# Half of the first slice's modulation product on TensorE with a one-column moving operand, between the transposes of x

## The chip, the cores and the metric

The kernel runs on one core of a Trainium2 chip. The metric is the time of one execution on the device in microseconds (us); smaller is better.

## The reference, cut to what matters

One decoder layer on 256 tokens of width 2048, in float32:

```python
mod = silu(c) @ w_ada + b_ada                       # (1, 2048) @ (2048, 6 * 2048)
sh1, sc1, g1, sh2, sc2, g2 = split(mod, 6)
h = rms_norm(x, norm1_gain) * (1.0 + sc1) + sh1
x = x + g1 * hybrid_mixer(h, ...)                   # begins with h @ w_in, 2048 x 16984
h = rms_norm(x, norm2_gain) * (1.0 + sc2) + sh2
x = x + g2 * swiglu(h, ...)
return rms_norm(x, final_norm_gain)
```

The change is in `silu(c) @ w_ada`, the product that makes the modulation, and there in a quarter of the columns of `sh1` and `sc1` alone. No other part of `w_ada` is touched.

## The kernel before

All large products run on TensorE with the contraction on the 128 partitions. A weight matrix comes from memory in chunks of four row tiles of 128 by 512 columns, 1 MB each. ScalarE casts a chunk, in halves, into its float32r part (`act.copy(hv, src)`, L303), VectorE subtracts that for the rest (L305), and TensorE makes three products for each row tile and token tile (L345 to L347): 24 for a chunk. The list `items` gives the order of the work, and `run()` walks through it; it also issues the loads on the SP queue in the order of the list, as far as there are free tiles named `raw`, three in each of two rings. A chunk is split two chunks ahead of its products.

The first products need `h`, and so the first norm and its modulation. To start early, the first 12 groups of `w_in` columns are done in four slices of four row tiles of the contraction (`INIT_KTS`), and each slice needs only its 512 columns of `sh1` and of `sc1`. Row 16p + j of `w_ada` lies on partition p. So a slice's part of `w_ada` is 16 rows for each partition, two times 512 columns wide, and it comes as eight pieces (`Ada`) of two rows `j` each, 1 MB, in two transfers of 512 KB, one for `sh1` and one for `sc1`. The tile `sc` holds silu(c) with a column for each `j`. VectorE works each piece into an accumulator `a`, by `pre_ada`: the product of a row with its column of `sc` (L283 for the very first row, a fused multiply-add L285 after it). What is left is a sum over the partitions, and the result must lie along partitions, as a column for each block of 128: `init_columns` calls `column_sums`, in which TensorE transposes the eight blocks of the accumulator (L481) and VectorE sums along the rows (L482). Three small VectorE operations (`mod_columns`, L455 to L457) make `A1` and `B1` of it.

Ahead of that stands the first norm (`first_norm`): ScalarE squares x and scales it in place (L451). Then `transpose_x` transposes it, 32 transposes of 128x128 on TensorE (L491), and ScalarE copies the result back in eight pieces (L495). `first_slice` then issues the casts of the first weight chunk (both halves, before all that follows on ScalarE), `init_columns`, and `init_modulate`, which makes `h` for four row tiles: ScalarE its float32r part (L464), VectorE a float32 copy (L468) and the rest (L471), with the halves of the first chunk's L305 between them.

Before the change the order at the start is: norm, all 32 transposes, the eight pieces (the last one worked segment by segment, `by_seg`, so that the transposes of the first segment can start early), `first_slice`, and the first products. The pieces of the later slices are spread between the groups of products.

Of the kernel before, what the change touches and what calls it, by code (L numbers as in the profile page):

```python
# [23 lines left out]
RAW_BUFS = 3          # raw chunks of weights in flight  # L24
EARLY_RAWS = 3        # and more of them while the working tiles of later stages are not there yet
HL_BUFS = 4           # halves of split chunks
AHEAD = 2             # chunks split ahead of their products
INIT_KTS = (4, 4, 4, 4)    # row tiles of the slices of the first products
ADA_DONE = 8          # the group of a slice before which the next slice's modulation is loaded and then applied
ADA_LEAD = (0, 2, 4)  # groups by which each slice's pieces of it start early  # L30
MID = 2               # row tile of the last chunk before which the first token tile's norm goes on
# The second norm's steps (512 columns, token tile) after the first two, with p for a half of a split,
# and the steps done before each row tile of the chunks that read them.
NORM_STEPS = "p 01 11 p p 20 21 30 31"
NORM_DONE = "0000 1233 3333 4557 7777 7777"
SLOT = 3.6            # vector engine time for the threads beside a chunk, in us
# [9 lines left out]
class Mm:  # L46
    """A chunk of a weight matrix: nk row tiles of 128, nc columns, for a group of products.

    With defer, the second token tile waits until a later chunk with by_token has done the first one.
    With home, its parts are in the tiles that home makes and not in the ring of all chunks.  # L50
    """
# [19 lines left out]
class Ada:  # L71
    """A piece of w_ada: nj of every partition's 16 rows, nc columns from c0 on of nseg segments."""

    def __init__(self, c0, nc, nseg, j0, nj, acc, pre=None):
        self.c0, self.nc, self.nseg, self.j0, self.nj, self.acc, self.pre = c0, nc, nseg, j0, nj, acc, pre
        self.by_seg = False

# [6 lines left out]
class Thread:  # L84
# [6 lines left out]
    def step(self):  # L91
        """The next step's cost, which it yields, or None at the end."""
        while True:
            if self.cur is None:
                if not self.q:
                    return None
                self.cur = self.q.popleft()
            try:
                return next(self.cur) or 0.0
            except StopIteration:  # L100
                self.cur = None
# [7 lines left out]
def tile_layer(tc, x, c, positions, norm1_gain, norm2_gain, w_ada, b_ada, w_in, gate_up, gate_bias,  # L109
# [3 lines left out]
    with (  # L113
# [42 lines left out]
        # ------------------------------------------------------------ constants and small inputs  # L156
# [36 lines left out]
        # rotary tables  # L193
# [22 lines left out]
        def rstd_of(ss, n, k):  # L216
            """(ss / n + eps) ^ -0.5 in place, k columns."""
            pool.tensor_scalar(ss, ss, 1.0 / n, EPS, ALU.mult, ALU.add)
            pool.tensor_tensor(ss, ss, half[:, 0:k], ALU.pow)

        def mean_of_three(ss):
            """ss[:, :, 0] becomes the part of mean + eps of the first three of four sums, for last_rstd."""
            pool.tensor_tensor(ss[:, :, 0], ss[:, :, 0], ss[:, :, 1], ALU.add)
            pool.tensor_tensor(ss[:, :, 0], ss[:, :, 0], ss[:, :, 2], ALU.add)
            pool.tensor_scalar(ss[:, :, 0], ss[:, :, 0], 1.0 / D, EPS, ALU.mult, ALU.add)
# [5 lines left out]
        # ------------------------------------------------------------ the stream of weights  # L231
# [42 lines left out]
        def pre_ada(it):  # L274
            if it.pre:
                it.pre()
            a = it.acc()
            segs = [slice(i, i + 1) for i in range(it.nseg)] if it.by_seg else [slice(0, it.nseg)]
            for g in segs:
                for j in range(it.nj):  # L280
                    s = sc[:, it.j0 + j:it.j0 + j + 1]
                    if it.j0 + j == 0:
                        dve.tensor_scalar_mul(a[:, g], it.raw[:, j, g], s)  # L283
                    else:
                        dve.scalar_tensor_tensor(a[:, g], it.raw[:, j, g], s, a[:, g], ALU.mult, ALU.add)  # L285
                    yield

        def pre_mm(it, rests_last=False):
            """The float32 chunk into its float32r part and the exact rest, a step for each half."""
            it.hl = []  # L290
            nk, ncol = (KT, 128) if isinstance(it, Lr) else (it.nk, it.nc)
            per = min(nk, 1024 // ncol)
            home = [h().rearrange("p (k n) -> p k n", k=nk) for h in getattr(it, "home", ())]
            rests = []
            for k in range(0, nk, per):
                src = it.raw[:, k:k + min(per, nk - k)]
                m = src.shape[1]
                if home:
                    hv, lv = (h[:, k:k + m] for h in home)
                else:  # L300
                    hv, lv = (stp.tile([128, 1024], F32R, tag=v, bufs=HL_BUFS, name=name(v))[:, 0:m * ncol]
                              .rearrange("p (k n) -> p k n", k=m) for v in ("hi", "lo"))
                act.copy(hv, src)  # L303
                it.hl.append((hv, lv))
                rests.append(lambda lv=lv, src=src, hv=hv: dve.tensor_sub(lv, src, hv.bitcast(F32)))  # L305
                if not rests_last:
                    rests.pop()()
                    yield
            for rest in rests:
                yield  # L310
                rest()

        def pre(its):
            """The pieces of its, a step of each in turn: steps of one piece of w_ada depend on each other."""
# [47 lines left out]
        def run():  # L362
# [36 lines left out]
            def pre_steps(**order):  # L399
                """The next chunk's pieces, a step at a time."""  # L400
# [38 lines left out]
        # ------------------------------------------------------------ first norm and its modulation  # L439
# [13 lines left out]
        def mod_columns(ps, n, A, B, bsc, bsh, gain):  # L453
            """A = (1 + scale) * gain and B = shift of n row tiles, from ps = [shift | scale]."""
# [4 lines left out]
        def modulated(kts, h, A, B, temp, on_act, between=None):  # L459
            """The transposed tokens in xs into the parts of h at the row tiles kts."""  # L460
# [14 lines left out]
        def column_sums(blocks, dst):  # L475
            """The sums of blocks [128, 128] over the partitions, a column of dst for each."""
# [7 lines left out]
        def transpose_x():  # L484
            """xs in place into its transposes, tiles [128, 256] for the row tiles; no block is overwritten before it is read."""
            pts = {}
            for k in range(0, KT, 2):
# [5 lines left out]
                for w in sorted(pts):  # L493
                    if min(2 * w + 4, KT) <= k + 2:
                        act.copy(xs[w // 8][:, (w % 8) * S:(w % 8 + 2) * S], pts.pop(w))  # L495

        def init_columns(s, k0, nk):
            a2 = init_acc(s, nk)
            pc = cp.tile([128, 2 * nk], F32, name=name("pc"))
            column_sums([a2[:, seg, a * 128:(a + 1) * 128] for seg in range(2) for a in range(nk)], pc)  # L500
# [48 lines left out]
        def first_transposes():  # L549
            first_norm()  # L550
            transpose_x()

        items.append(Call(first_transposes))
        items.extend(init_ada(*slices[0]))
        items[-1].by_seg = True
# [32 lines left out]
        # ------------------------------------------------------------ gated linear attention  # L588
# [179 lines left out]
        # ------------------------------------------------------------ indexer  # L768
        def rope(v, nh, dh, rot, step):
            """Rotates the first rot of dh in each of nh heads, in place, on both token tiles."""  # L770
# [100 lines left out]
        # ------------------------------------------------------------ sparse attention  # L871
# [3 lines left out]
        def seg_start(i):  # L875
            """Before the first piece of a segment: what the last one left is reduced."""
# [20 lines left out]
        def reduce_rows(dst, n):  # L897
            """A slice of 512 of the sums over the partitions added to dst, on every partition."""
# [112 lines left out]
        # ------------------------------------------------------------ branches, gates and merge  # L1011
# [32 lines left out]
        def split_transposes(src, kt0, dst):  # L1044
            """Transposes [128, 2, 512] into row tiles kt0.. of the parts in dst, in two steps."""
# [94 lines left out]
        # ------------------------------------------------------------ second norm  # L1140
        def second_norm(last):
# [17 lines left out]
            def modulate(n, t, ps, a0, na):  # L1159
                """Row tiles of one token tile; the second token tile's products are on the other engine."""  # L1160
# [61 lines left out]
        # ------------------------------------------------------------ feed-forward  # L1222
# [55 lines left out]
        def final_token(t):  # L1278
            """The last norm of a token tile; the columns before the last 512 have their gain already."""
# [54 lines left out]
def constants():  # L1334
    """Constants of the shapes alone: the identity, the masks of the decay's levels, the rotary frequencies."""
# [37 lines left out]
```

## Time and profile before

| what | value |
|---|---|
| time, median of 3 runs (lowest to highest) | 1889.79 us (1889.21 to 1892.36) |
| span of the profiled execution, first to last instruction | 1885.6 us |
| median less that span | 4.2 us |
| TensorE, busy share of the span | 97% |
| VectorE, ScalarE, GpSimd | 68%, 45%, 7% |
| memory traffic, mean over the span | 233 GB/s |
| granted TensorE clock, mean over the span | 0.995 of full speed |

The trace gives the span only; what lies around it in the execution's own time is not in the profile, so the last difference is taken for it. A busy time is the time in which an engine had an instruction in work. Times in the trace count from the first instruction.

### The profile page before, as it was taken

To read this page: it belongs to the slowest core of one execution; us is meant where nothing else is said; L and a number is where in the kernel's file an instruction comes from. 1 tells how busy PE (TensorE), PEld (TensorE's weight loads), DVE (VectorE), ACT (ScalarE), POOL (GpSimd) and SP (SyncE) were. 2 spreads that over 40 slices of the span, in tenths; PEclk is the share of its full clock that TensorE was granted. 3 is DMA by queue.
4 is the path that set the end of the run, shared out by engine and by line. 5 is a ranking of instruction groups with operands and counts; after the bars stand their busy time and mean duration, and the time that the engine had idled before them with its cause. 6 is when DMAs were issued, how large, how long until landed. Compare 5 with 4: busy or idle time off the path is not lost.

```text
span 1885.6 us, 23215 instructions
## 1 busy us (share of the span) xinstructions
PE 1834.9 (97%) x9148; PEld 1510.9 (80%) x9148; DVE 1286.0 (68%) x1442; ACT 854.0 (45%) x1115; POOL 138.3 (7%) x201
## 2 busy tenths in 40 slices
PE   3999999999999999999999999999999999999998
PEld 3888888777788888888888787888788888888886
DVE  6899865788866678777777656677555444554455
ACT  4554444655645444344344446444333444334443
POOL 0000000543220110200000000000000000000002
PEclk8999999999999999999999999999999999999999
DMA  9998843543444787878888754888555555555553
GB/s 369 387 345 315 282 161 104 182 154 135 150 164 156 270 298 280 300 269 300 305 312 312 275 193 164 318 328 314 178 200 191 189 189 191 186 194 194 185 180 133
DMA packets 198046, 440.84 MB, mean 234 GB/s; under 512 B 7816, under 2 KB 14112, under 8 KB 188848
## 3 DMA queue, kind: packets, MB, share of 16 engines
q1 hardware_dynamic: 196544, 433.69, 65.5%
q10 hardware_dynamic: 1392, 5.66, 0.8%
q8 instruction: 72, 1.18, 0.2%
q14 instruction: 38, 0.31, 0.0%
HBM read 437.22 MB, written 2.10 MB: 233 GB/s over the span
## 4 chain that ended last, share of the span: by engine, by line
PE 78%; issue 12%; DVE 3%; POOL 3%; ACT 2%; DMA 1%; SPq 0%; POOLq 0%; ACTq 0%; DVEq 0%
PE pm L345 25%; PE pm L347 25%; PE pm L346 25%; DVE acc L285 1%; PE pa L1050 1%; DVE lo L305 1%; ACT hi L303 1%; POOL tm L782 1%; POOL rp L783 1%; POOL rp L780 0%; POOL rp L781 0%; PE ph L679 0%; POOL rp L779 0%; DMA raw<-in_w_ada_dram 0%; PE pa L901 0%
## 5 line engine op out<-in xcount | busy, mean ns | idle before, releaser
L305 DVE TENSOR_TENSOR lo<-raw,hi 128x1024 fp32r<-128x1024 f32 (+1 forms) x632 | 768.0, 1225 | 537.1 <-ACT hi L303 536.7
L303 ACT CAST hi<-raw 128x1024 fp32r<-128x1024 f32 (+1 forms) x632 | 652.6, 1041 | 898.8 <-PE pm L347 714.6
L345 PE MATMUL pm<-hi,h 128*128 128x512 f32 (+1 forms) x1784 | 699.0, 392 | 2.2 <-ACT h L464 1.9
L347 PE MATMUL pm<-hi,h 128*128 128x512 f32 (+1 forms) x1784 | 690.5, 387 | 0.0
L346 PE MATMUL pm<-lo,h 128*128 128x512 f32 (+1 forms) x1784 | 689.6, 387 | 0.2 <-DVE lo L305 0.2
L345 PEld LDWEIGHTS pm<-hi,h 128*128 128x128 f32 x1784 | 335.9, 188 | 70.1 <-ACT h L464 2.3
L347 PEld LDWEIGHTS pm<-hi,h 128*128 128x128 f32 x1784 | 335.5, 188 | 68.9 <-DVE h L471 0.2
L346 PEld LDWEIGHTS pm<-lo,h 128*128 128x128 f32 x1784 | 336.0, 188 | 66.1 <-DVE lo L305 0.9
L345 PE MATMUL pm<-hi,gA 128*128 128x512 f32 x608 | 242.1, 398 | 0.0
L347 PE MATMUL pm<-hi,gB 128*128 128x512 f32 x608 | 237.0, 390 | 0.0
L346 PE MATMUL pm<-lo,gA 128*128 128x512 f32 x608 | 236.8, 389 | 0.1
L285 DVE SCALAR_TENSOR_TENSOR acc<-raw,sc,acc 128x2048 f32<-128x2048 f32 (+2 forms) x122 | 218.2, 1789 | 3.5 <-DMA raw<-in_w_ada_dram 2.6
L346 PEld LDWEIGHTS pm<-lo,gA 128*128 128x128 f32 x608 | 114.2, 188 | 25.1 <-issue 1.7
L345 PEld LDWEIGHTS pm<-hi,gA 128*128 128x128 f32 x608 | 114.2, 188 | 24.7 <-issue 1.9
L347 PEld LDWEIGHTS pm<-hi,gB 128*128 128x128 f32 x608 | 114.1, 188 | 24.2
L1274 POOL TENSOR_TENSOR gC<-gC,gr 128x512 f32<-128x512 f32 x3 | 4.9, 1640 | 716.9 <-ACT pm L1272 716.9
L663 POOL TENSOR_TENSOR acc<-gC 128x512 f32<-128x512 f32 x32 | 40.0, 1260 | 34.0 <-DVE acc L672 33.6
L672 DVE TENSOR_TENSOR acc<-gB,acc 128x256 f32<-128x256 f32 x64 | 32.3, 565 | 6.9 <-ACT acc L667 6.8
L779 POOL TENSOR_TENSOR rp<-tm,cos 128x64 f32<-128x64 f32 x18 | 12.2, 677 | 297.8 <-ACT tm L927 180.1
L981 ACT ACTIVATE S<-S,mx 128x128 f32<-128x128 f32 (+1 forms) x32 | 14.3, 448 | 32.8 <-DVE mx L979 32.8
L667 ACT ACTIVATE acc<-acc 128x256 f32<-128x256 f32 x64 | 22.3, 416 | 9.7 <-POOL acc L663 9.6
L345 PE MATMUL pm<-hi,gr 128*128 128x512 f32 x64 | 24.9, 389 | 0.0
(271 smaller groups left out, 1066.6 us busy)
## 6 DMA issues: line engine op xcount, KB each, us to landing
raw<-in_w_in_dram SPq DMA_DIRECT2D x129, 1024.0 KB, 4.9
raw<-in_w_ffn_gate_up_dram SPq DMA_DIRECT2D x88, 1024.0 KB, 4.9
raw<-in_w_ada_dram SPq DMA_DIRECT2D x64, 1024.0 KB, 4.8
raw<-in_w_ffn_down_dram SPq DMA_DIRECT2D x44, 1024.0 KB, 5.2
raw<-in_w_ada_dram SPq DMA_DIRECT2D x64, 512.0 KB, 8.5
raw<-in_w_branch_gla_dram SPq DMA_DIRECT2D x16, 1024.0 KB, 5.3
raw<-in_w_branch_dsa_dram SPq DMA_DIRECT2D x16, 1024.0 KB, 5.3
raw<-in_w_merge_out_dram SPq DMA_DIRECT2D x16, 1024.0 KB, 5.4
```

The lines of the kernel that those rows point to most:

```text
L285: dve.scalar_tensor_tensor(a[:, g], it.raw[:, j, g], s, a[:, g], ALU.mult, ALU.add)
L303: act.copy(hv, src)
L305: rests.append(lambda lv=lv, src=src, hv=hv: dve.tensor_sub(lv, src, hv.bitcast(F32)))
L345: pe.matmul(o, a, hv, start=it.first and k == 0, stop=False)
L346: pe.matmul(o, a, lv, start=False, stop=False)
L347: pe.matmul(o, b, hv, start=False, stop=it.last and k == it.nk - 1)
L663: pool.tensor_tensor(d, v, v[:, :, s - 1:s].to_broadcast([128, n, 2 * s]), ALU.subtract)
L667: act.activation(d, d, AF.Exp, scale=(1.0 if u else -1.0) / 16)
L672: dve.tensor_tensor(w, src, d, ALU.mult)
L782: pool.tensor_tensor(a, u[0], u[1], ALU.subtract)
L783: pool.tensor_tensor(u[0], b, co, ALU.mult)
L1050: pe.transpose(ps[:, a * S + t * 128:a * S + t * 128 + 128], src[:, t, (i * 2 + a) * 128:(i * 2 + a + 1) * 128], ident)
```

## The change

In each of the eight pieces of the first slice the row `j = 0` stays on VectorE, and the row `j = 1` goes to TensorE (`on_pe = (1,)`). For it each block of 128 by 128 of the piece is the stationary operand, and the column of `sc` is the moving operand, one column wide. Eight such products for each piece (two segments, four blocks) add up in eight columns of one PSUM tile, `state["pc"]`, taken at the start with `psum_held`. In `init_columns` of the first slice the eight blocks of VectorE's accumulator are multiplied by a column of ones into the same eight columns, in place of the eight transposes and two sums. `by_seg` goes. The 32 transposes of x, which stood ahead of all pieces in TensorE's order, now come in four bursts of eight, after the second, third, fourth and fifth piece. The later slices and all else stay as they are. The rest of the difference between the files is comments.

```diff
 class Ada:
...
         self.by_seg = False
+        self.on_pe = ()
...
                 for j in range(it.nj):
                     s = sc[:, it.j0 + j:it.j0 + j + 1]
+                    if j in it.on_pe:
+                        for i in range(2):
+                            for k in range(it.nc // 128):
+                                c = i * it.nc // 128 + k
+                                pe.matmul(state["pc"][:, c:c + 1], it.raw[:, j, i, k * 128:(k + 1) * 128], s,
+                                          start=c == 0 and it.j0 + j == it.on_pe[0], stop=False)
+                        continue
                     if it.j0 + j == 0:
                         dve.tensor_scalar_mul(a[:, g], it.raw[:, j, g], s)
...
         def transpose_x():
             pts = {}
+            yield
             for k in range(0, KT, 2):
...
                         act.copy(xs[w // 8][:, (w % 8) * S:(w % 8 + 2) * S], pts.pop(w))
+                yield
 
         def init_columns(s, k0, nk):
             a2 = init_acc(s, nk)
-            pc = cp.tile([128, 2 * nk], F32, name=name("pc"))
-            column_sums([a2[:, seg, a * 128:(a + 1) * 128] for seg in range(2) for a in range(nk)], pc)
+            blocks = [a2[:, seg, a * 128:(a + 1) * 128] for seg in range(2) for a in range(nk)]
+            if s == 0:
+                pc = state["pc"]
+                for i, b in enumerate(blocks):
+                    pe.matmul(pc[:, i:i + 1], b, ones[:, 0:1], start=False, stop=i == 2 * nk - 1)
+            else:
+                pc = cp.tile([128, 2 * nk], F32, name=name("pc"))
+                column_sums(blocks, pc)
...
-        def first_transposes():
+        def first_steps():
+            state["pc"] = psum_held()
             first_norm()
-            transpose_x()
-
-        items.append(Call(first_transposes))
-        items.extend(init_ada(*slices[0]))
-        items[-1].by_seg = True
+            state["x_steps"] = transpose_x()
+            next(state["x_steps"])
+
+        items.append(Call(first_steps))
+        for i, it in enumerate(init_ada(*slices[0])):
+            it.on_pe = (1,)
+            items.append(it)
+            if 1 <= i <= 4:
+                items.append(Call(lambda: [next(state["x_steps"]) for _ in range(2)]))
         items.append(Call(first_slice))
```

## Rows read from the trace of the kernel before

**Rows 1.** The page: the chain that ended last, shares of the span

```profile
PE 78%; issue 12%; DVE 3%; POOL 3%; ACT 2%; DMA 1%; SPq 0%; POOLq 0%; ACTq 0%; DVEq 0%
```

**Rows 2.** Stages: window, length, busy (count) of five engines, clock, DMA share, GB/s

```profile
12.00:37.50 25.50, 8.19 (x40) 6.91 (x40) 22.64 (x25) 10.82 (x14) 2.95 (x5) 0.85 1.05 388
37.50:44.00 6.50, 6.31 (x15) 4.71 (x16) 6.29 (x12) 3.44 (x5) 0.00 (x0) 0.53 1.05 386
...
50.00:100.00 50.00, 50.00 (x226) 41.49 (x226) 40.87 (x41) 29.76 (x41) 0.00 (x0) 1.00 1.02 374
```

**Rows 3.** VectorE in order of time, 11 to 44 us: start, length, instruction

```profile
12.16 0.75 DVE L283 TENSOR_SCALAR acc<-raw,sc 128x1024 f32<-128x1024 f32 x1 [4.16 <-DMA raw<-in_w_ada_dram]
...
15.27 19.16 DVE L285 SCALAR_TENSOR_TENSOR acc<-raw,sc,acc 128x1024 f32<-128x1024 f32 x16 [1.03 <-DMA raw<-in_w_ada_dram]
34.34 0.69 DVE L482 TENSOR_REDUCE pc<-pa 128x4 f32<-128x512 f32 x1
...
36.30 0.15 DVE L455 TENSOR_TENSOR mods<-pc,cols 128x4 f32<-128x4 f32 x1
...
36.62 0.16 DVE L457 SCALAR_TENSOR_TENSOR mods<-mods,cols 128x4 f32<-128x4 f32 x1
...
41.85 0.43 DVE L471 TENSOR_TENSOR h<-mod,h 128x256 fp32r<-128x256 f32 x1
...
42.85 1.22 DVE L305 TENSOR_TENSOR lo<-raw,hi 128x1024 fp32r<-128x1024 f32 x1
```

**Rows 4.** ScalarE in order of time, 11 to 85 us

```profile
34.10 1.99 ACT L303 CAST hi<-raw 128x1024 fp32r<-128x1024 f32 x2 [7.04 <-DMA raw<-in_w_in_dram]
...
36.87 2.08 ACT L464 ACTIVATE h<-gB,mods 128x256 fp32r<-128x256 f32 x4 [0.78 <-DVE mods L457]
...
73.27 2.00 ACT L303 CAST hi<-raw 128x1024 fp32r<-128x1024 f32 x2 [2.45 <-DMA raw<-in_w_in_dram]
...
78.69 2.00 ACT L303 CAST hi<-raw 128x1024 fp32r<-128x1024 f32 x2 [2.45 <-DMA raw<-in_w_in_dram]
```

**Rows 5.** TensorE in order of time, 11 to 38 us

```profile
19.05 0.90 PE L491 MATMUL pa<-cc,gB 128*128 128x128 f32 x3 [1.42 <-ACT gB L451]
...
20.60 1.06 PE L491 MATMUL pa<-cc,gB 128*128 128x128 f32 x4
...
23.12 0.60 PE L491 MATMUL pm<-cc,gB 128*128 128x128 f32 x4
23.56 0.60 PE L491 MATMUL pa<-cc,gB 128*128 128x128 f32 x4
...
34.57 1.08 PE L481 MATMUL pa<-cc,acc 128*128 128x128 f32 x4 [0.36 <-DVE acc L285]
37.52 0.80 PE L345 MATMUL pm<-hi,h 128*128 128x512 f32 x1 [1.87 <-ACT h L464]
```

**Rows 6.** TensorE's waits for others, 40 to 320 us: total, times, longest

```profile
PE pm L345 <- DVE gr L529: 0.3, 1, 0.3
```

**Rows 7.** Weight loads and matmuls of three lines: ns min/median/max, starts, shapes

```profile
L901 PEld LDWEIGHTS pa<-acc,ones x16: 187/188/190, 1061.9 to 1357.1; 128*128 128x128 f32 x16
L901 PE MATMUL pa<-acc,ones x16: 592/592/593, 1062.2 to 1357.5; 128*128 128x512 f32 x16
...
L679 PEld LDWEIGHTS ph<-acc x640: 105/113/114, 380.3 to 526.6; 128*32 128x32 f32 x160
...
L345 PEld LDWEIGHTS pm<-hi,h x6: 187/330/330, 37.5 to 43.9; 128*128 128x128 f32 x6
...
L345 PEld LDWEIGHTS pm<-hi,h x73: 187/188/190, 50.1 to 99.9; 128*128 128x128 f32 x73
```

**Rows 8.** Three single microseconds, columns as in the stages

```profile
35.00:36.00 1.00, 0.65 (x4) 0.25 (x2) 0.33 (x2) 1.00 (x2) 0.00 (x0) 0.50 1.05 385
...
42.00:43.00 1.00, 1.00 (x4) 0.74 (x3) 1.00 (x3) 0.00 (x0) 0.00 (x0) 0.50 1.05 387
43.00:44.00 1.00, 1.00 (x5) 0.82 (x4) 1.00 (x2) 0.00 (x0) 0.00 (x0) 0.73 1.04 383
```

More of the change, by code (lines that the diff above doesn't have):

```diff
@@ L27 @@
 AHEAD = 2
-INIT_KTS = (4, 4, 4, 4)
+INIT_KTS = (4,4,4,4)
 ADA_DONE = 8
```

## The prediction

> **What bounds the kernel now.** I read first the chain of work that ended last, then the stages, and then the first 45 us engine by engine.
>
> The chain runs 78% on TensorE and 1% on transfers [rows 1]. From 50 us on TensorE has no free microsecond in the stage shown [rows 2], and between 40 and 320 us it waits once for another engine, 0.3 us [rows 6]. So the time is the moment of the first product plus a stream that runs without pause, and the change touches only what lies ahead of that moment. A microsecond lost there stays lost; one gained stays gained as long as weights come in time.
>
> The first product starts at 37.52 [rows 5]. Backwards from it: `h` at 36.87, released by VectorE [rows 4]; the three small operations from 36.30 to 36.78; two sums over the transposed accumulator, the first at 34.34; before that 16 fused multiply-adds in 19.16 us without a gap [rows 3]. This train on VectorE is what the change halves.
>
> Two other things end almost as late. Transfers run at 388 GB/s through all of this [rows 2], so a piece of 1.05 MB takes 2.7 us: the first was there at 12.16 [rows 3], and the first weight chunk, which follows the eighth piece in the queue, at 34.10 [rows 4], hence the eighth piece at about 31.4. No order of the engines' work makes that earlier. And the two casts of that chunk stand ahead of `h` on ScalarE and end at 36.09; `h` waited only 0.78 us beyond them [rows 4]. So from a quicker modulation at most 0.8 us can come.
>
> **What is taken off VectorE.** Eight rows of 1.28 us (19.16 us for 16, the last four of half width) go, and `by_seg` with them: some 10 us of work. VectorE then waits for transfers: it ends its last row 1.28 us after 31.4, at 32.7. The two sums of 0.69 us [rows 3] and the eight transposes, of which the second four start at 34.57 [rows 5], go too. The transfers keep their order. A `raw` tile now comes free only when TensorE has read it too, and SP's later issues wait for that; the queue is so far ahead (the eighth piece is in it long before it lands) that a microsecond there costs nothing.
>
> **What is put on TensorE.** Per piece eight products, and eight at the end for the accumulator: 72 calls. The trace has no call with one moving column, so I build it from loads and bound it.
>
> A float32 call of L901 shows as two loads and two matmuls: 16 of each for its eight calls [rows 7]. So 144 loads of 128x128. At the fast clock a load of 32 columns takes 0.113 us and one of 128 columns 0.188 [rows 7]: 0.075 for 96 columns, so 128 columns stream in 0.10 us, and 0.09 is fixed and overlaps the load before. With one moving column nothing else fills the array, and loads follow each other: 0.21 us a call at the fast clock. At the slow clock the same load takes 0.33 (the median up to 44 us, [rows 7]); the streaming part doubles, 0.42 us a call. The lower bound is one visible load a call, 0.21 even at the slow clock; the upper bound is no overlap, twice 0.33 = 0.66.
>
> The transposes cost 1.55 us for seven at the slow clock (19.05 to 20.60), 0.22 each, and 0.44 for four at the fast one (23.12 to 23.56), 0.11 each [rows 5]: 1.75 or 0.88 us a burst of eight.
>
> TensorE works in order, so the first burst, which needs x scaled at 19.05 [rows 5], also holds up the third piece, and each later piece waits for a burst. At the slow clock, with 3.36 us for eight calls: first and second piece 12.2 to 18.9; from 19.05 four bursts (7.0), six pieces and the columns (seven times 3.36, 23.5): end at 49.55. No wait for transfers is in it, since each piece takes longer than the 2.7 us between two of them. With 0.2 us until the last matmul is through and 0.48 for the small operations, `A1` and `B1` stand at 50.2. From there to the first product it took 0.74 us before (36.78 to 37.52), so it comes at 51.0, 13.4 us later than now.
>
> At the fast clock, 1.68 us for eight calls: the sixth piece ends at 19.05 + 4 x 0.88 + 4 x 1.68 = 29.3, the seventh at 31.0, the eighth waits until 31.4 and ends at 33.1, the columns at 34.8, `A1` at 35.5: ahead of the casts. Between these two lies the case. Break-even is a call of 0.18 us with slow transposes (19.05 + 7.0 + 56 x 0.18 = 36.1) or of 0.24 with fast ones.
>
> **Which clock.** Transposes back to back brought the high level, 2.4 GHz: their spacing falls from 0.22 to 0.11 [rows 5]. So did products back to back: 0.50 of it at 42 us, 0.73 in the microsecond after [rows 8]. The transposes of the accumulator, in two groups with a gap, did not: at 35 us the level is 1.2 GHz and stays there [rows 8]. A stretch of loads, each followed by one column, is none of these. I take the slow level: it is the one at which the transposes at 19.05 began [rows 5], and the dense stretches that are known to raise it are now cut into four bursts with 3.4 us between them. That is a choice, and the largest doubt here.
>
> The Trainium skill ("TensorE: Matmul & The Clock Gate", section "LDWEIGHTS (loading the stationary operand)") gives a load as its columns divided by 1.2, in ns, whatever the gate lets through. That is 107 ns for 128 columns, an estimate by that page of 0.21 us a call at either clock; the sum with slow transposes would be the 1.7 us loss of the third rival below. The rows speak against it: the same load took 0.188 us at one level and 0.33 at the other [rows 7].
>
> **The forecast:** 1885.6 of the profile + 13.4 = 1899.0, and with the 4.2 us by which the median of the runs lies above that span, 1903.
>
> **The rivals.**
>
> *The clock rises in the first pieces and stays up* (not slower). The calls alone keep TensorE occupied from 12.2 us on, and if that brings the high level as the dense rows did, TensorE keeps pace with the transfers. `h` starts with the end of the casts, 0.8 us earlier. Then the first chunk also runs at the high level. Now 15 products had started by 44.0 and the other nine follow at 0.22 (226 in 50 us [rows 2]), so the chunk ends at 46.1 and the next, 24 more, at about 51.5. With the high level VectorE's last rest of `h` bounds the first chunk (41.85 + 0.43, less 0.9) and the rest of the next chunk (42.85 + 1.22, less 0.9 [rows 3]) the second, which would end at 43.2 + 5.4 = 48.6. The gain is 2.9 us, time 1887. More is not to be had: chunks land 5.42 us apart (73.27 and 78.69 [rows 4]), TensorE uses one in 5.4, and the ninth, landing at 78.69 and split by 81.0, is used from 46.1 + 7 x 5.44 = 84.2, with 3.2 us in hand. It decides at 0.24 us a call. For it speaks that TensorE has no gap after 19 us; against it, that no row shows loads alone raising the level.
>
> The Trainium skill (same page, Part 1 on the clock gate) says that activity releases the throttle and that "The HW doesn't count instructions". By that rule a steady stream of calls would do, and this rival's 1887 would be the time; no row here shows such a stream.
>
> *A call costs one load in time*, the second hidden, at the slow clock: 19.05 + 7.0 + 7 x 1.68 = 37.8, first product at 39.2, a loss of 1.7: 1891. For it speaks only that pairs of loads are not seen apart in the trace.
>
> *Loads do not overlap*, 0.66 a call: the second piece ends at 22.7, all at 66.7, a loss of 30: 1920. Against it: in the dense stream products follow each other at 0.22 with loads of 0.188 beside them.
>
> *The weights after the pieces starve*: with the slow calls tiles come free up to 20 us later than now, and transfers pause. But the chunks issued then land before 51 and the second chunk is not needed before 59. It adds nothing unless a call is far above 0.42.
>
> **How the numbers follow.** The forecast has 0.56, the risen clock 0.27, one load a call 0.09, no overlap or a mixture above 1908 0.08. Predicted is 1903; the likeliest case's own range is 1899 to 1908, from a call of 0.36 to 0.50. The range 1886 to 1908 takes in the risen clock and leaves out the last case and the ends. 0.2% is 3.8 us, about what a measurement of this kernel can tell from no change. Faster by that needs more than the risen clock gives: 0.03. Within it are most of the risen clock, the one-load case and the least of the forecast: 0.36. Slower: 0.61.
>
> **What would show it.** Per piece some 16 loads over 3.4 us (forecast) or 1.7 (rival); the granted clock between 12 and 50 us; the first L345 at 51 or at 36.8; VectorE idle between its eight rows, waiting for transfers; the wait of the small operations for TensorE, which is near nothing now. The prediction is wrong if the clock rises before 25 us, or if a call costs less than 0.24.

## The result and the profile after

The changed kernel takes 1901.76 us, the median of five runs (1901.01 to 1903.10), against 1889.79 us for five runs of the kernel before (1887.59 to 1893.44): a ratio of 1.0057, 95% interval 1.0044 to 1.007, or 8.3 to 13.2 us more. The forecast was 1903.0 in a range of 1886 to 1908, slower. The profiled execution is the one of 1901.01 us, and its span is 1899.2. In nearly every execution on record the time is 1.7 to 1.9 us more than the span. So of the 4.2 us between the median and the span of before, about 1.8 lie around the span, and the rest is that the traced execution of before was faster than the median.

The page of the changed kernel: the chain's shares, and the calls' group among the costliest.

```profile
PE 80%; issue 13%; POOL 3%; DVE 2%; ACT 2%; DMA 0%; POOLq 0%; ACTq 0%; DVEq 0%
...
L287 PEld LDWEIGHTS ph<-sc,raw 128*128 128x128 f32 x128 | 27.9, 333 | 3.2 <-ACT pm L453 3.2
```

TensorE gains 2 points of the chain, VectorE loses 1 [rows 1]. The new group is 128 loads, 27.9 us in all. Where they lie is seen in order of time, TensorE, 10 to 58 us:

```profile
10.92 6.96 PE L287 MATMUL ph<-sc,raw 128*128 128x1 f32 x32 [3.07 <-ACT pm L453]
17.74 1.09 PE L500 MATMUL pa<-cc,gB 128*128 128x128 f32 x4
18.62 1.06 PE L500 MATMUL pm<-cc,gB 128*128 128x128 f32 x4
19.48 3.41 PE L287 MATMUL ph<-sc,raw 128*128 128x1 f32 x16
22.75 1.09 PE L500 MATMUL pa<-cc,gB 128*128 128x128 f32 x4
...
34.52 10.24 PE L287 MATMUL ph<-sc,raw 128*128 128x1 f32 x48
44.62 3.55 PE L513 MATMUL ph<-ones,acc 128*128 128x1 f32 x16
49.38 0.80 PE L353 MATMUL pm<-hi,h 128*128 128x512 f32 x1 [1.21 <-ACT h L472]
...
54.35 0.51 PE L354 MATMUL pm<-lo,h 128*128 128x512 f32 x1
54.70 0.40 PE L355 MATMUL pm<-hi,h 128*128 128x512 f32 x1
```

From the first call at 10.92 on no wait stands in brackets until the columns end at 48.2. The pattern of 16 matmuls and eight transposes repeats until the last three pieces come together at 34.52, then the columns. The first product starts at 49.38, 11.9 us after that of before [rows 5]. VectorE and ScalarE in order of time show who now waits for whom:

```profile
15.31 1.28 DVE L293 SCALAR_TENSOR_TENSOR acc<-raw,sc,acc 128x1024 f32<-128x1024 f32 x1 [1.92 <-DMA raw<-in_w_ada_dram]
...
32.89 1.28 DVE L293 SCALAR_TENSOR_TENSOR acc<-raw,sc,acc 128x1024 f32<-128x1024 f32 x1 [2.75 <-DMA raw<-in_w_ada_dram]
48.21 0.16 DVE L463 TENSOR_TENSOR mods<-ph,cols 128x4 f32<-128x4 f32 x1 [14.04 <-PE ph L513]
```

```profile
36.94 2.03 ACT L311 CAST hi<-raw 128x1024 fp32r<-128x1024 f32 x2
48.73 2.07 ACT L472 ACTIVATE h<-gB,mods 128x256 fp32r<-128x256 f32 x4 [9.76 <-DVE mods L465]
```

VectorE's train without gaps [rows 3] has become eight rows that each wait for a transfer, and then VectorE waits 14.04 us for TensorE. `h`, which waited 0.78 us beyond the casts [rows 4], waits 9.76. The bound of this stage has moved from VectorE to TensorE.

Two stages, and what TensorE waits for between 52 and 330 us:

```profile
12.00:20.00 8.00, 8.00 (x40) 7.97 (x40) 3.32 (x3) 4.34 (x4) 1.74 (x5) 1.00 1.05 389
...
50.00:54.00 4.00, 3.83 (x10) 2.93 (x10) 3.79 (x9) 2.69 (x4) 0.00 (x0) 1.00 0.00 0
```

```profile
PE pm L353 <- DVE gr L545: 0.3, 1, 0.3
```

The column of the granted clock reads 1.00 in both stages although loads take 333 ns; the last section says why it is not trusted so near the start, and the level is read from durations here. The transfers do stand still (0 GB/s from 50 to 54 us), but after the first products TensorE waits for no weights: one wait of 0.3 us, the same as before [rows 6]. The loss is passed on. The transposes of q and k, the mixer's queries and keys, are a later stage of TensorE's work; their line before and after:

```profile
L613 PE MATMUL pa<-cc,gC x16: 270/272/273, 311.2 to 320.9; 128*128 128x128 f32 x16
```

```profile
L634 PE MATMUL pa<-cc,gC x16: 271/272/273, 322.7 to 332.4; 128*128 128x128 f32 x16
```

They start 11.5 us later. The other 0.4 us are won back inside the first chunk, whose 24th product starts at 57.47 against 45.98. At the end the two spans differ by 13.6 us, and the medians by 12.0: the traced execution of after loses some 2 us more far behind the change, shown with the two mixtures below.

### The profile page after: what moved, and what is told of

Read it like the earlier page. It is cut to its first block, busy times and chain, and to the rows that moved or that the text cites. A ratio compares the mean times of both kernels' runs of the same rounds, so it can differ in the third digit from the quotient of the medians.

```text
span 1899.2 us, 23476 instructions
## 1 busy us (share of the span) xinstructions
PE 1866.6 (98%) x9284; PEld 1542.9 (81%) x9284; DVE 1273.5 (67%) x1430; ACT 854.5 (45%) x1115; POOL 135.6 (7%) x201
## 4 chain that ended last, share of the span: by engine, by line
PE 80%; issue 13%; POOL 3%; DVE 2%; ACT 2%; DMA 0%; POOLq 0%; ACTq 0%; DVEq 0%
PE pm L353 25%; PE pm L355 24%; PE pm L354 24%; PE ph L287 1%; PE pa L1071 1%; DVE lo L313 1%; ACT hi L311 1%; POOL tm L803 0%; POOL rp L802 0%; POOL rp L801 0%; POOL rp L804 0%; POOL rp L800 0%; DVE acc L693 0%; PE pa L922 0%; DMA gB<-in_x_dram 0%
## 5 line engine op out<-in xcount | busy, mean ns | idle before, releaser
L293 DVE SCALAR_TENSOR_TENSOR acc<-raw,sc,acc 128x2048 f32<-128x2048 f32 (+1 forms) x112 | 207.3, 1851 | 14.0 <-DMA raw<-in_w_ada_dram 14.0
L693 DVE TENSOR_TENSOR acc<-gB,acc 128x256 f32<-128x256 f32 x64 | 31.4, 551 | 7.3 <-ACT acc L688 7.2
L287 PEld LDWEIGHTS ph<-sc,raw 128*128 128x128 f32 x128 | 27.9, 333 | 3.2 <-ACT pm L453 3.2
L287 PE MATMUL ph<-sc,raw 128*128 128x1 f32 x128 | 27.4, 348 | 3.1 <-ACT pm L453 3.1
```

What stands on the lines that cost most here:

```text
L287: pe.matmul(state["pc"][:, c:c + 1], it.raw[:, j, i, k * 128:(k + 1) * 128], s, start=c == 0 and it.j0 + j == it.on_pe[0], stop=False)
L693: dve.tensor_tensor(w, src, d, ALU.mult)
```

## The experiments

The first four ran beside 26 runs of the kernel before (median 1889.75), the last three beside 23 (1889.15). "First product" is the start of the first line L345 (before) or its counterpart.

**Wide calls (e1_wide).** The same 72 calls with the same stationary blocks, but the moving column repeated to 128 columns: 128 times the arithmetic, the same number of loads. The results lie in two tiles of PSUM, of which one column in 128 is read. (The diff is cut: the columns of ones are widened in the same way.)

```diff
-    pe.matmul(state["pc"][:, c:c + 1], it.raw[:, j, i, k * 128:(k + 1) * 128], s, ...)
+    pe.matmul(state["pc"][i][:, k * 128:(k + 1) * 128], it.raw[:, j, i, k * 128:(k + 1) * 128],
+              s.to_broadcast([128, 128]), ...)
```

> The change, with a moving operand of 128 equal columns instead of one in all 72 calls (two PSUM banks in place of eight columns): 128 times the arithmetic, the same loads. Theory (the calls run at the slow clock because a stream of loads with one column behind each does not raise it): the array now streams, the clock rises within the first pieces, a call falls from 0.42 to about 0.21 us, the first product comes at about 36.8 us instead of 49.4 and the time is about 1888. Rival A (a load of a float32 block takes 0.21 us at any clock in such a stream, so loads bound it): no faster than the change, first product at 49 or later, 1901 or more. Rival B (order: the pieces wait behind the bursts): also 1901.

Measured: 1888.5 us, ratio 0.9992 [0.9983, 1.0001]; first product at 38.35. TensorE in order of time, and then the loads by line:

```profile
11.35 2.04 PE L286 MATMUL ph<-sc,raw 128*128 128x128 f32 x8 [3.77 <-DMA raw<-in_w_ada_dram]
...
14.89 1.11 PE L286 MATMUL ph<-sc,raw 128*128 128x128 f32 x8
15.84 1.05 PE L286 MATMUL pa<-sc,raw 128*128 128x128 f32 x8
```

```profile
L286 PEld LDWEIGHTS ph<-sc,raw x64: 186/191/333, 11.3 to 32.5; 128*128 128x128 f32 x64
```

The pace doubles between 14.9 and 15.8, in the second piece; from then on eight matmuls take 0.89 us (18.30 to 19.19 in the trace), 0.111 a load, and the median load is 191 ns. More arithmetic made the same loads faster and took the whole 12 us away. The first product is 1.6 us later than I expected, because the first weight chunk came late: its cast starts at 35.80 here, at 34.10 before [rows 4].

**One burst (e2_block).** All 32 transposes after the second piece, so that one dense stretch raises the level; six pieces of one-column calls and the columns follow.

```diff
-            if 1 <= i <= 4:
-                items.append(Call(lambda: [next(state["x_steps"]) for _ in range(2)]))
+            if i == 1:
+                items.append(Call(lambda: [next(state["x_steps"]) for _ in range(8)]))
```

> The change, with all 32 transposes of x in one block after the second piece instead of four bursts of eight. Theory: the block raises the clock as the same block did before the change (after some 4 us), so that half of the transposes and the next pieces run at the high level; the calls alone do not hold it, and it falls back about 5 us after the last transpose, as it did before. Pieces three to six then take 1.7 us each and the rest 3.4: first product at about 41, time about 1893. Rival A (calls hold the level once it is up): all pieces keep pace with the transfers, first product at about 36.8, 1888. Rival B (the cost is not the clock): 1901 as with four bursts.

Measured: 1897.29 us, 1.0034 [1.0021, 1.0047]; first product at 43.67. TensorE, and then single microseconds (columns as in [rows 2]):

```profile
19.75 1.06 PE L500 MATMUL pa<-cc,gB 128*128 128x128 f32 x4
20.61 0.69 PE L500 MATMUL pm<-cc,gB 128*128 128x128 f32 x4
...
22.88 16.17 PE L287 MATMUL ph<-sc,raw 128*128 128x1 f32 x96
38.91 3.55 PE L513 MATMUL ph<-ones,acc 128*128 128x1 f32 x16
43.67 0.79 PE L353 MATMUL pm<-hi,h 128*128 128x512 f32 x1 [1.22 <-ACT h L472]
```

```profile
26.00:27.00 1.00, 1.00 (x11) 1.00 (x10) 0.49 (x1) 0.00 (x0) 0.00 (x0) 1.00 1.12 406
27.00:28.00 1.00, 1.00 (x9) 1.00 (x9) 0.79 (x1) 0.00 (x0) 0.00 (x0) 0.80 0.98 369
28.00:29.00 1.00, 1.00 (x6) 1.00 (x6) 0.00 (x0) 0.00 (x0) 0.00 (x0) 0.50 1.05 385
```

The transposes double their pace at 20.6 and the calls after them run at 0.11 a load; then, with TensorE without a gap, the granted clock falls from 1.00 to 0.50 within the microsecond from 27, and the same line goes on at 0.21 a load. I had counted on four fast pieces; from 22.88 to about 27.7 at 0.111 there are some 44 loads, 2.75 pieces. The other 1.25 pieces, at 3.4 us instead of 1.7, are 2.1 us of the miss of 2.7. One-column calls did not hold the level here.

**Half as many calls (e3_four).** Only every second piece has its second row on TensorE, the other four are whole on VectorE. (The flag that starts the sum in PSUM moves to the new first call.)

```diff
-            it.on_pe = (1,)
+            it.on_pe = (1,) if i % 2 else ()
```

> The change, with the row j = 1 of only four of the eight pieces (the second, fourth, sixth and eighth) on TensorE and VectorE doing both rows of the others. Theory (the number of calls at 0.42 us sets the end, TensorE in order): calls and bursts from 15.3: burst one and two to 22.1, fourth piece to 25.5, bursts three and four to 29.0, sixth piece to 32.4, eighth to 35.8, the columns to 39.2, first product at about 40.5, 3 us later than before the change: about 1893. Rival (the place of the bursts or the added waits set it, not the number of calls): stays near 1901.

Measured: 1886.75 us, 0.9988 [0.9978, 0.9997]; first product at 38.12, 2.4 us ahead of what I expected. TensorE:

```profile
17.16 1.43 PE L500 MATMUL pa<-cc,gB 128*128 128x128 f32 x4
...
20.94 2.00 PE L287 MATMUL ph<-sc,raw 128*128 128x1 f32 x16
...
24.59 0.97 PE L287 MATMUL ph<-sc,raw 128*128 128x1 f32 x8
25.86 1.05 PE L287 MATMUL ph<-sc,raw 128*128 128x1 f32 x8 [0.30 <-DMA raw<-in_w_ada_dram]
29.93 3.57 PE L287 MATMUL ph<-sc,raw 128*128 128x1 f32 x16 [3.01 <-DMA raw<-in_w_ada_dram]
33.36 3.55 PE L513 MATMUL ph<-ones,acc 128*128 128x1 f32 x16
```

I had priced all calls at the low level. But the third piece has no calls here, so two bursts of transposes stand together from 17.16 to 20.9, and the level rises in the piece behind them: 16 matmuls in 2.00 us instead of 3.41. The granted clock falls within the wait of 3.01 us (0.55 in the microsecond from 28), and the eighth piece runs at the low level. So the level of a piece's calls depends on what stands ahead of them. The first product is 0.6 us later than in the trace of before [rows 5], and yet the median is 3.0 us lower. The spans of the two traced executions differ by 1.5 us. The pace of the first chunk doubles sooner here (its 24th product starts at 45.42 against 45.98), which leaves 0.5 at the transposes of q and k; another 1.1 come between 625 and 890 us, where one wait for GpSimd is 1.0 us long instead of 2.5. The rest of the 3.0 comes from where the two traced executions lie among the others.

**Only the columns (e4_columns).** No piece on TensorE; the bursts, the columns of ones and the absence of `by_seg` stay. With no calls between them the four bursts run as one block again on TensorE, from 17.06 to 24.9, so this run says nothing of cutting the block into bursts. (The start flag moves here too.)

```diff
-            it.on_pe = (1,)
+            it.on_pe = ()
```

> No piece on TensorE, all rows on VectorE as before the change, but the rest of the change kept: bursts between the pieces, no segment-by-segment last piece, and the eight products with a column of ones in place of eight transposes and two sums. Theory: VectorE ends its rows at about 34.1, eight calls of 0.42 take 3.4 us, first product at about 38.8, 1.3 us later than before the change: about 1891, so that nearly all of the 12 us lies in the 64 calls for the pieces. Rival (the new end of the first slice or the moved transposes cost most of it): 1896 or more.

Measured: 1890.71 us, 1.0008 [0.9999, 1.0017]; first product at 38.51. TensorE:

```profile
33.76 3.54 PE L513 MATMUL ph<-ones,acc 128*128 128x1 f32 x16 [8.88 <-DVE acc L293]
38.51 0.79 PE L353 MATMUL pm<-hi,h 128*128 128x512 f32 x1 [1.21 <-ACT h L472]
```

The new end of the slice costs 1.0 us of the 11.9: eight one-column calls (3.54 us) against eight transposes, two sums and what lay between. The other 10.9 come with the 64 calls among the pieces and the cut into bursts that they bring.

**Filling TensorE in the kernel before (e5_fill).** The kernel before, with 70 transposes of the identity behind those of x and 14 behind those of the accumulator, into a tile of PSUM that nobody reads.

```diff
+        def fill(n):
+            for i in range(n):
+                pe.transpose(state["fill"][:, (i % 4) * 128:(i % 4 + 1) * 128], ident, ident)
...
             column_sums([a2[:, seg, a * 128:(a + 1) * 128] for seg in range(2) for a in range(nk)], pc)
+            if s == 0:
+                fill(14)
...
             transpose_x()
+            fill(70)
```

> The kernel before the change, with 70 transposes of the identity after those of x and 14 after the eight of the accumulator, whose result nobody reads. Theory (the clock alone makes the first chunk slow): the level is up from 23 us to the first products, the column sums and the first 15 products run at 0.11 and 0.23 instead of 0.21 and 0.43; the first product stays at about 37.3 and the first chunk ends 2 to 3 us sooner, bounded by VectorE's rests of h: about 1887.3. Rival (VectorE or the weights set the first chunks anyway): no gain, 1889.8.

Measured: 1883.71 us, 0.9971 [0.996, 0.9982]: 3.4 to 7.6 us faster than the kernel before, and the only one of all whose ratio lies more than 0.2% below 1. TensorE:

```profile
24.48 7.80 PE L500 MATMUL ph<-cc 128*128 128x128 f32 x70
32.67 0.63 PE L481 MATMUL pa<-cc,acc 128*128 128x128 f32 x4 [0.38 <-DVE acc L285]
...
34.59 1.69 PE L500 MATMUL ph<-cc 128*128 128x128 f32 x14
37.50 0.50 PE L345 MATMUL pm<-hi,h 128*128 128x512 f32 x1 [1.22 <-ACT h L464]
37.84 0.40 PE L346 MATMUL pm<-lo,h 128*128 128x512 f32 x1
```

The first product starts when it did before [rows 5], but from the second on products follow each other at 0.23. The 24th starts at 42.88, in the trace of before at 45.98. Of these 3.1 us 3.0 are still there at the transposes of q and k (308.2 against 311.2), and the spans of the two traced executions differ by 3.5. The medians differ by 5.4, and again the traced execution of before is one of its fast ones: its span is 1885.6, that of the median run 1887.4. What makes the other executions of before slower, no trace shows.

**Two mixtures (e6_four_wide, e7_wide_fill).** The first is e3_four with wide calls and with 30 idle transposes after the sixth piece and 10 after the columns; the second is e1_wide with 12 idle transposes between the columns and the first product.

On top of e3_four with wide calls (`first_fill` issues the 30 transposes), and on top of e1_wide, both cut:

```diff
+            if i == 5:
+                items.append(Call(first_fill))
...
                     pe.matmul(pc[i // nk][:, i % nk * 128:(i % nk + 1) * 128], b, ones, ...)
+                fill(10)
```

```diff
                     pe.matmul(pc[i // nk][:, i % nk * 128:(i % nk + 1) * 128], b, ones, ...)
+                state["fill"] = psum_main()
+                fill(12)
```

> The version with four pieces shared, with 128 equal moving columns in all calls, 30 transposes of the identity after the sixth piece and 10 after the column sums. Theory: calls and columns at 0.22 us throughout; the eighth piece's calls end at about 32.4, VectorE at 32.7, the columns at 34.5, h starts with the end of the two casts at 36.0, first product at 36.6 and at the high level: 3 us less than before, about 1886, under both kernels and a little under the four-piece version. Rival (the first slice is bounded elsewhere, by the weights or VectorE after h): first product no earlier than 37.5, about 1888.

> The change with 128 equal moving columns, and 12 transposes of the identity between the column sums and the first product. Theory: what was left to gain there was the clock that fell at 39 us; with the gap filled the first eight products run at 0.23 instead of 0.43, about 1.5 us less than without: about 1887. Rival (the products of the first chunk wait for VectorE's rests): 1888.5, no change.

Measured: 1889.37 us, 1.0002 [0.9993, 1.0011], first product at 38.52; and 1886.69 us, 0.9987 [0.9978, 0.9996], first product at 37.39. The second is what I expected. The first is a miss: the weights' cast starts only at 35.97, so the first product is 1.9 us late. At the transposes of q and k the first stands at 309.5 and the second at 308.3, ahead of before (311.2) by 1.7 and 2.9 us. In the profiled executions (1890.22 and 1889.95 us, the latter the slowest of the 11 of e7_wide_fill) both lose that again between 625 and 890 us: 267.7 and 268.8 us for a stretch that took 264.2 before. In after (637 to 904 us) it took 266.5. TensorE waits for GpSimd's rotary products there, 5.4 and 5.5 us in all against 3.7, and 4.1 in after. The rest is the clock. The longest of these waits, and two microseconds behind it, in before, e7_wide_fill and after:

```profile
802.85 0.55 PE L944 MATMUL pa<-cc,tm 128*128 128x128 f32 x3 [2.46 <-POOL tm L784]
804.00:806.00 2.00, 2.00 (x10) 1.63 (x9) 2.00 (x2) 0.00 (x0) 0.00 (x0) 1.00 0.80 336
```

```profile
803.04 0.90 PE L973 MATMUL pa<-cc,tm 128*128 128x128 f32 x3 [2.67 <-POOL tm L813]
804.00:806.00 2.00, 2.00 (x6) 1.52 (x6) 2.00 (x2) 0.00 (x0) 0.00 (x0) 0.50 0.69 291
```

```profile
815.46 0.65 PE L965 MATMUL pa<-cc,tm 128*128 128x128 f32 x3 [2.91 <-POOL tm L805]
816.00:818.00 2.00, 2.00 (x6) 1.56 (x6) 1.85 (x2) 0.00 (x0) 0.00 (x0) 0.50 1.08 388
```

Behind the wait the granted clock is at 0.50 in after and in both mixtures, and stays at 1.00 in before. From the first product there to the twelfth it takes 2.6 us in before, 4.2 in e6_four_wide and in after, and 4.8 in e7_wide_fill. With the longer waits this makes 3.3 of the 3.5 us lost in e6_four_wide, 4.0 of the 4.6 in e7_wide_fill and 2.0 of the 2.3 in after. Why the level fell in these executions and not in that of before is open: in e1_wide it fell (0.50 from 804 to 806 us) behind a wait of 2.46 us, as long as that of before.

## Why the prediction was right

**The bound and the passing on.** Right: of the 11.9 us at the first product 11.5 are left at the transposes of q and k, and the medians differ by 12.0. That the traced span, 1899.2, meets the forecast 1899.0 is luck: the first product came 1.6 us early, and some 2 us were lost at 815 us, where the prediction had nothing.

**Two loads a call, 0.42 us.** Right. By line, the loads of the pieces and of the columns in the changed kernel:

```profile
L287 PEld LDWEIGHTS ph<-sc,raw x128: 287/333/337, 10.9 to 44.3; 128*128 128x128 f32 x128
...
L513 PEld LDWEIGHTS ph<-ones,acc x16: 333/333/333, 44.5 to 47.8; 128*128 128x128 f32 x16
```

128 loads for 64 calls, 333 ns each, as the 330 of the low level before [rows 7]. The last three pieces and the columns, 64 loads from 34.52 to 48.2, follow each other at 0.213 us: 0.427 a call, 3.41 a piece where I had 3.36. The derivation from loads of 32 and of 128 columns came out, though its parts do not add up at the low level: 0.09 and a doubled 0.10 make 0.29, where the row has 0.33. The spacing of loads is what it had right. The rival of one visible load and that of no overlap (0.66) are both out.

The Trainium skill ("TensorE: Matmul & The Clock Gate", section "LDWEIGHTS (loading the stationary operand)") has one formula for a load, its columns divided by 1.2 in ns, with no second one for the other level; 128 columns make 107 ns. The pace agrees with it at the high level (0.111 in e1_wide and e2_block) and not at the low one (0.213 here). By that figure the sum came to the loss of 1.7 us of the rival of one load a call, which is the second in the prediction's list and not the third.

**The choice of the clock.** Right, and now shown. The calls of after run 37 us at the pace of the low level, and four bursts of eight transposes do not raise it. e1_wide changes only the width of the moving operand (and with it the PSUM tiles), and the pace doubles. e2_block and e3_four bring the level up with dense transposes. In e2_block the one-column calls then lose it without any gap, and there the granted clock and the pace are seen to change together: 1.00 with 0.11 a load, 0.50 with 0.21. In e3_four it falls in a wait, which shows nothing of the calls. The rival in which the level rises was about right on its price, 1887: e1_wide, where the level falls again at 38.9 us, takes 1888.5, and e7_wide_fill, where it stays up for the first products, 1886.69.

The Trainium skill (same page, Part 1 on the clock gate) has activity release the throttle and says that "The HW doesn't count instructions". No run here tests how the chip measures activity. What they show is that TensorE without an idle moment for 37 us, with one-column matmuls and bursts of eight transposes, stayed at the low level.

**The mis-sized term.** The first product came at 49.38, not 51.0. From the first burst to the end of the columns I had 30.5 us and it took 30.4 (17.74 to 48.17): calls and bursts are right. The step that is off is "first and second piece 12.2 to 18.9; from 19.05 four bursts". The calls began at 10.92 and not at 12.2: they need only the first segment of the piece, and VectorE waits for both (in e1_wide TensorE is released by that transfer at 11.35, VectorE at 12.70). And x was scaled earlier: I took 19.05 from before [rows 5], but the change moved that too. GpSimd's steps of the norm in order of time, in the kernel before and then after:

```profile
12.26 0.70 POOL L448 TENSOR_TENSOR s<-s 128x2 f32<-128x2 f32 x1
13.06 1.23 POOL L218 TENSOR_SCALAR s<-s 128x2 f32<-128x2 f32 x1
```

```profile
12.36 0.19 POOL L456 TENSOR_TENSOR s<-s 128x2 f32<-128x2 f32 x1
12.65 0.19 POOL L219 TENSOR_SCALAR s<-s 128x2 f32<-128x2 f32 x1
```

The same two operations on two columns take 1.93 us beside VectorE's rows and 0.38 us where VectorE still waits for its first piece or has only just begun; the third, L219 and now L220, takes 0.70 and 1.02. The last step of the norm ends at 13.94 instead of 15.07, the scaling starts at 13.98 instead of 15.11, and the first burst at 17.74: 1.3 us earlier than forecast. The other 0.3 us are the small operations: 1.2 from the last column to the first product, where I had 1.45.

**What hides the rest.** Right: late `raw` releases cost nothing. SP waited 19.5 us for TensorE's reads up to 45 us (12.1 ahead of pieces, 7.4 ahead of weight chunks), and the transfers paused, yet no product waited for weights. The 4.2 us between the span and the median was in part a property of that one execution (for the changed kernel the median lies 2.6 above its span), and it made the sum comparable with the median.

**What stays open.** The landing of the first weight chunk (the start of its cast) varies from 33.62 in e4_columns over 34.10 before to 35.97 in e6_four_wide. Where TensorE shares the pieces and it is late, one interval between two pieces is longer than 2.7 us, with transfers at 385 to 390 GB/s: 4.2 in e1_wide and e6_four_wide, 3.2 in e2_block and e7_wide_fill. In after it is 4.0, so that VectorE's last row started at 32.89, where the prediction had the eighth piece at 31.4. I did not find its cause. It bounds every version whose modulation is early enough. Each version has one trace, so how much of this is the version and how much the execution is open too.

## What to carry to other kernels

A matmul with one moving column cost its weight loads here, in float32 two of them a call, and a nearly idle TensorE was at the low level, where they cost double: price them from rows at the level that the new work will see, and read that level from what stands ahead of it. Moving work from VectorE to a waiting TensorE can pay only if its calls fit between the transfers at that level. Where a dense stage follows an idle stretch, dense work of no use ahead of it can be worth more than the work moved: 3.0 us here where the traces show it, and 3.4 to 7.6 in the times.

## What the hardware showed unexpectedly

- Loads with one-column matmuls, and bursts of eight transposes among them, did not raise the level in 37 us of unbroken work, and one-column calls alone did not hold it: in e2_block it fell in the microsecond from 27 without a gap. The same calls 128 columns wide were twice as fast from between 14.9 and 15.8 us on.
- The clock column of the stages reads 1.00 from 12 to 20 us and from 50 to 54 us in the changed kernel, where loads take 333 ns, four transposes 0.88 us and products 0.43, the pace of the low level. It seems to stand at full until the first change is recorded; at the start of a trace the level is better read from durations.
- Small GpSimd operations took 0.70 and 1.23 us beside VectorE's rows, and 0.19 us where VectorE waited or had just begun. With all rows back on VectorE (e4_columns) they took 0.73 and 1.23 again, and x was scaled as late as before.
- Behind a wait of 2.46 us for GpSimd at about 803 us TensorE went on at 1.00 in before and at 0.50 in e1_wide. The lower level cost 1.6 to 2.2 us in the three executions measured above, hundreds of microseconds behind the change.
